# Local operand of a state-space mixer from half-row products of C, and quarter 3's first products moved ahead of the scan's end

## The chip, the cores and the metric

The kernel runs on one core of a Trainium2 chip. The metric is the device time of one execution in microseconds; a kernel is run several times and the median counts. Beside that, one execution is recorded by the hardware profiler, and all rows below come from that record of the kernel before.

## What is computed

The program is a small two-layer network on 256 tokens of width 2048, in float32: a state-space (S5) mixer with a gated projection, a feed-forward block, a dilated-window attention layer, and a second feed-forward block. The change lies in the mixer alone. Cut to what matters, it is, for each of 128 groups of 16 channels with 64 complex states:

```
def step(carry, u_c):                       # a chunk of the sequence
    bu = einsum('blgh,gph->blgp', u_c, bb)  # input into the states (complex)
    _, s = associative_scan(combine, (a, bu), axis=1)
    st = a_cum * carry + s                  # states over time
    y = einsum('blgp,ghp->blgh', st_re, cr) - einsum('blgp,ghp->blgh', st_im, ci)
    return st[:, -1], y
y = y + d_skip * u
g = gelu(y)
val, gate = split(g @ w_glu)
out = val * sigmoid(gate)
```

## The kernel before

The mixer handles the sequence as 64 short chunks of 4 tokens, and the 128 groups as four quarters (`qr` 0 to 3). Inside a chunk the answer is a fixed linear map of the chunk's own inputs, the *local operand* `mt`; across chunks a state is carried by a serial scan of 63 steps on VectorE (`scan`), one chain for quarters 0 and 1 (`sa`) and one for quarters 2 and 3 (`sb`). The output of a quarter is the sum of *local products* (`y_local`: inputs `ub` times `mt`) and *state products* (`y_state`: scanned states `sts` times `fds`, which GpSimd prepares), in two PSUM tiles. State products can be made for chunks 0 to 31 (early half) before the scan has ended, and for chunks 32 to 63 (late half) behind its end.

The work stands in one order written out by hand (`T`, `A`, `G`, `W` are TensorE, ScalarE, GpSimd and VectorE with that order kept). Every engine runs its own queue in order.

`build_m(qr)` makes a quarter of `mt`. It multiplies the taps `gps[qr]` (128 rows: two halves of 64, one for each half `y` of a pair of groups) with the output matrix `cp`, real and imaginary part in turn, and adds the skip term (`dsm`, through the identity `ident`). The two halves must not mix, so ScalarE first writes copies of `cp` in which the other half's rows are zero (`m_operand`, tile `cb`, through `masks`), and each product has 128 rows and 2 x 32 columns. ScalarE then copies the sum into `mt`, and SyncE sends six small transfers that shift it for the other three tokens of a chunk (line 477).

Behind it come the local products of quarters 0 and 1, their early state products, those of quarter 2, and then, as the chain goes on: late state products of quarters 0 and 1, gelu on ScalarE, a transpose (`turn`), a high and a low part of the result (`low`, VectorE), and the first products with the gated projection's weights (`feed`). `feed(1, 1)` is the last of those ahead of the end of `sb`; then late state products of quarter 2, all of quarter 3, and the rest.

PSUM is held in three pools: `ps_mm` (4 tiles), `ps_tr` (2), `ps_ms` (2). The scan keeps tables in two tiles of `ps_mm` until it has ended. Line 59 is the helper through which all ordered instructions pass, so tiles tell them apart, not lines.

Of the kernel before, what the change touches and what calls it, by code (L numbers as in the profile page):

```python
# [12 lines left out]
FP32 = mybir.dt.float32  # L13
F32R = mybir.dt.float32r
I32 = mybir.dt.int32
AF = mybir.ActivationFunctionType
# [4 lines left out]
P = 128  # L21
# [8 lines left out]
GI = 16  # L30
NS = 64
# [30 lines left out]
class Net:  # L62
# [141 lines left out]
    def s5_glu(self):  # L204
# [242 lines left out]
            for k in range(2):  # L447
                pair(cp[:, k, mo:mo + 16], cf[:, k, :, mo:mo + 16], ct[:, :, mo:mo + 16])

        def m_operand(qr, j4):  # L450
            m0 = 16 * qr + 8 * j4
            cb = early.tile([P, 2, 4, 2, 32], FP32, name="cb", tag="cb", bufs=2)
            src = cp[:, :, m0:m0 + 8].rearrange("p r (j x) o -> p r j (x o)", x=2)
            for y in range(2):
                A.activation(out=cb[:, :, :, y], in_=src, func=AF.Copy, scale=masks[:, y:y + 1])
            return cb

        def build_m(qr):
            cbs = [m_operand(qr, j4) for j4 in range(2)]
            ps = self.ps_ms.tile([P, 8, 2, 2, GI], FP32, name="ms")  # L460
            for xx in range(2):
                T.matmul(ps[:, :, :, xx], lhsT=self.ident,
                         rhs=dsm[:, 16 * qr:16 * qr + 16].rearrange("p (j y) o -> p j y o", y=2),
                         start=(xx == 0), stop=False, skip_group_check=True)
            for j in range(8):
                for ri in range(2):
                    T.matmul(ps[:, j], lhsT=gps[qr][:, ri, 2 * j:2 * j + 2].rearrange("p x s i -> p (x s i)"),
                             rhs=cbs[j // 4][:, ri, j % 4].rearrange("p y c -> p (y c)"),
                             start=False, stop=(ri == 1), skip_group_check=True)
            mo = 16 * qr  # L470
            for xx in range(2):
                r = slice(64 * xx, 64 * xx + 64)
                A.copy(out=mt[r, 3, mo:mo + 16].rearrange("p (j y) o -> p j y o", y=2), in_=ps[r, :, :, xx])
            for t in range(3):
                n = 16 * (t + 1)
                for xx in range(2):
                    nc.sync.dma_start(out=mt[64 * xx:64 * xx + n, t, mo:mo + 16],
                                      in_=mt[64 * xx + 64 - n:64 * xx + 64, 3, mo:mo + 16])
# [31 lines left out]
        def y_local(qr, pool, nm):  # L510
            pss = [pool.tile([P, 8, 4, GI], FP32, name=nm) for _ in range(2)]
            for jq in range(8):
                for y in range(2):
                    for xx in range(2):
                        T.matmul(pss[y][64 * xx:64 * xx + 64, jq],
                                 lhsT=ub[qr // 2][:, (qr % 2) * 8 + jq, y, xx],
                                 rhs=mt[:, :, 2 * (8 * qr + jq) + y],
                                 start=(jq == 0), stop=False, skip_group_check=True)
            return pss

        def y_state(qr, pss, jqs=range(8), c0=0, c1=64):
            st, mo = sts[qr // 2], 16 * (qr % 2)
            for jq in jqs:
                for ri in range(2):
                    for xx in range(2):
                        for y in range(2):
                            r = slice(64 * y, 64 * y + 64)
                            T.matmul(pss[y][64 * xx + c0:64 * xx + c1, jq],
                                     lhsT=st[r, c0:c1, ri, mo + 2 * jq + xx],
                                     rhs=fds[qr][r, :, ri, 2 * jq + xx],  # L530
                                     start=False, stop=(ri == 1), skip_group_check=True)
# [78 lines left out]
        def rest(c, half):  # L610
            r, hi, lo = ws[c, half]
            tt(lo, r, hi.bitcast(FP32), ALU.subtract, W)

        def feed(c, half):
            r, hi, lo = ws.pop((c, half))
            self.products(gb0, [(hi[:, k], lo[:, k]) for k in range(2)], lhs, T)
# [3 lines left out]
        def turn(qr, j4):  # L620
            if qr % 2 == 0 and j4 == 0:
                gtile[qr // 2] = self.act_tile()
                lhs.extend(gtile[qr // 2][:, k] for k in range(8))
            pt = self.ps_ms.tile([P, 4, 2, NS], FP32, name="ms")
            for t in range(4):
                T.transpose(out=pt[:, t], in_=gms[qr][:, j4, t].rearrange("p j y o -> p (j y o)"),
                            identity=self.ident)
            for xx in range(2):
                hi = lhs[4 * qr + 2 * j4 + xx][:, 0].rearrange("p (c t) -> p t c", t=4)
                A.copy(out=hi, in_=pt[:, :, xx])  # L630
            return pt
# [39 lines left out]
        feed(1, 0)  # L671
        high(2, 0)
        feed(1, 1)
        rest(2, 0)
        y_state(2, yl[2], range(8), 32, 64)
        high(2, 1)
        rest(2, 1)
        gms[2] = gelu(yl[2])
        yl[3] = y_local(3, self.ps_mm, "mm")
        y_state(3, yl[3])  # L680
        turns(2)
        gms[3] = gelu(yl[3])
        feed(2, 0)
# [333 lines left out]
```

## Time and profile before

| | |
|---|---|
| median of 3 runs | 2430.44 us (2430.07 to 2431.36) |
| profiled execution | 2428.69 us |
| its span | 2426.9 us |
| TensorE busy | 2392.5 us, 99% of the span |
| VectorE, ScalarE, GpSimd busy | 55%, 45%, 5% |

The span is the time from the first to the last recorded instruction; the profiled execution's own time has 1.8 us around it. A product of two float32 operands appears in the trace as two weight loads (LDWEIGHTS, engine row PEld) and two multiplications (MATMUL, row PE). A form such as `64*128 64x128` means a tile of the array of 64 rows and 128 columns, and an operand of 64 partitions and 128 elements.

### The profile page before, as it was taken

The numbers are of one execution on the slowest core, as the hardware profiler recorded it, in microseconds if no ns is written. First come the engines' busy times: TensorE is split into PE (matmuls) and PEld (weight loads), VectorE is DVE, ScalarE is ACT, GpSimd is POOL, SyncE is SP. The second block draws the span as 40 slices with busy tenths as digits, with TensorE's granted clock in tenths as the row PEclk, the third lists the DMA queues.
The fourth block names the chain that finished last, engine by engine and source line by source line (L and its number), as shares of the span: only waits on it lengthen the run. The fifth ranks groups of instructions, "written<-read, shape, count | busy, mean of one in ns | idle before, by whom it ended". The sixth has DMA issues, their size and how long they took to land.

```text
span 2426.9 us, 29373 instructions
## 1 busy us (share of the span) xinstructions
PE 2392.5 (99%) x11856; PEld 1936.8 (80%) x11856; DVE 1323.8 (55%) x1974; ACT 1081.4 (45%) x1367; POOL 113.5 (5%) x113
## 2 busy tenths in 40 slices
PE   6899999999999999999999999999999999999999
PEld 5788888888888888888888888788888888888887
DVE  8955454454444454565446676765454444454454
ACT  7344444444334444554445555554444433344433
POOL 4800000000000000000000000100000000000000
PEclk9899999999999999999999999999999999999999
DMA  2345555555555555555554444445555555555554
GB/s 85 96 163 185 181 189 180 185 191 176 189 191 187 179 188 182 182 194 181 184 184 170 156 156 142 156 154 185 182 188 179 185 191 187 184 184 188 179 197 148
DMA packets 63033, 423.58 MB, mean 175 GB/s; under 512 B 8112, under 2 KB 9520, under 8 KB 12336
## 3 DMA queue, kind: packets, MB, share of 16 engines
q1 hardware_dynamic: 61744, 419.60, 50.7%
q8 instruction: 93, 1.52, 0.3%
q10 hardware_dynamic: 1152, 2.10, 0.2%
q14 instruction: 44, 0.36, 0.0%
HBM read 418.79 MB, written 2.10 MB: 173 GB/s over the span
## 4 chain that ended last, share of the span: by engine, by line
PE 97%; DVE 2%; ACT 1%; issue 0%; DMA 0%; POOL 0%; SPq 0%; DVEq 0%; POOLq 0%
PE mm L122 30%; PE mm L124 30%; PE mm L123 30%; PE ms L59 2%; PE tr L59 1%; PE ms L857 1%; PE tr L743 1%; PE mm L59 1%; PE tr L808 1%; DVE mm L59 0%; PE tr L857 0%; PE tr L185 0%; DVE gp L59 0%; DVE gpb L59 0%; PE ms L887 0%
## 5 line engine op out<-in xcount | busy, mean ns | idle before, releaser
L104 DVE TENSOR_TENSOR wlo<-raw,whi 128x1024 fp32r<-128x1024 f32 x776 | 948.5, 1224 | 1003.6 <-ACT whi L103 1002.1
L103 ACT CAST whi<-raw 128x1024 fp32r<-128x1024 f32 x776 | 813.0, 1048 | 1161.9 <-PE mm L124 1142.2
L122 PE MATMUL mm<-whi,actt 128*128 128x512 f32 x3104 | 1235.8, 398 | 1.4 <-ACT whi L103 1.4
L124 PE MATMUL mm<-whi,actt 128*128 128x512 f32 x3104 | 1229.6, 396 | 0.0
L123 PE MATMUL mm<-wlo,actt 128*128 128x512 f32 x3104 | 1229.3, 396 | 0.0
L124 PEld LDWEIGHTS mm<-whi,actt 128*128 128x128 f32 x3104 | 583.1, 188 | 139.2
L122 PEld LDWEIGHTS mm<-whi,actt 128*128 128x128 f32 x3104 | 583.1, 188 | 138.3 <-ACT whi L103 2.1
L123 PEld LDWEIGHTS mm<-wlo,actt 128*128 128x128 f32 x3104 | 583.2, 188 | 136.9 <-DVE wlo L104 0.4
L795 POOL TENSOR_TENSOR sc<-ssq,mhalf 128x8 f32<-128x8 f32 x16 | 32.1, 2005 | 475.0 <-DVE ssq L793 475.0
L174 POOL TENSOR_TENSOR r<-m,mhalf 128x1 f32<-128x1 f32 x6 | 3.2, 552 | 1053.1 <-DVE m L173 848.9
L59 DVE TENSOR_TENSOR actr<-actr,mm 128x64 f32<-128x64 f32 x252 | 46.7, 215 | 2.0
L729 ACT ACTIVATE sg<-mm,r 128x512 f32<-128x512 f32 x44 | 30.1, 690 | 21.3 <-PE mm L124 21.0
L59 DVE TENSOR_TENSOR mm<-mm,actr 128x128 f32<-128x128 f32 x126 | 37.0, 294 | 0.9
L866 ACT ACTIVATE s<-s,mx 128x384 f32<-128x384 f32 (+1 forms) x32 | 24.8, 774 | 25.1 <-DVE mx L864 25.1
L59 POOL TENSOR_TENSOR fpr<-pf,cp 128x512 f32<-128x512 f32 x32 | 34.9, 1092 | 0.0
L733 DVE SCALAR_TENSOR_TENSOR sg<-mm,r,sg 128x512 f32<-128x512 f32 x44 | 30.9, 742 | 0.0
L59 ACT COPY actr<-ms 128x252 f32<-128x252 f32 (+1 forms) x40 | 19.9, 580 | 22.5 <-PE ms L59 21.4
L791 ACT ACTIVATE sq<-mm 128x512 f32<-128x512 f32 x32 | 19.0, 594 | 23.5 <-PE mm L124 23.5
L871 DVE SCALAR_TENSOR_TENSOR p<-s,z,p 128x128 f32<-128x128 f32 (+1 forms) x64 | 26.3, 411 | 3.8 <-ACT p L869 3.6
L747 DVE TENSOR_TENSOR actt<-tr,actt 128x512 fp32r<-128x512 f32 x44 | 28.2, 681 | 0.0
L746 ACT CAST actt<-tr 128x512 fp32r<-128x512 f32 x44 | 23.7, 590 | 10.1 <-PE tr L743 10.1
L743 PEld LDWEIGHTS tr<-ident,sg 128*128 128x128 f32 x176 | 19.4, 140 | 9.2 <-DVE sg L733 9.2
(180 smaller groups left out, 946.8 us busy)
## 6 DMA issues: line engine op xcount, KB each, us to landing
raw<-w_gu SPq DMA_DIRECT2D x176, 1024.0 KB, 4.8
raw<-w_down SPq DMA_DIRECT2D x88, 1024.0 KB, 4.8
raw<-w_q SPq DMA_DIRECT2D x48, 1024.0 KB, 4.8
raw<-w_glu SPq DMA_DIRECT2D x32, 1024.0 KB, 4.8
raw<-w_kv SPq DMA_DIRECT2D x32, 1024.0 KB, 4.7
raw<-w_o SPq DMA_DIRECT2D x16, 1024.0 KB, 4.7
actr<-x_c SPq DMA_DIRECT2D x2, 1024.0 KB, 6.4
xr<-x_t SPq DMA_DIRECT2D x8, 256.0 KB, 5.8
```

The costliest lines, as they stand in the source:

```text
L59: return lambda *a, **k: self.tc.keep_in_program_order(call(*a, **k))
L103: (scalar or self.nc.scalar).copy(out=hi, in_=r)
L104: (vector or self.nc.vector).tensor_tensor(out=lo, in0=r, in1=hi.bitcast(FP32), op=ALU.subtract)
L122: matmul(ps[th], lhsT=a[:, 0, ts], rhs=hi, start=(k == 0), stop=False)
L123: matmul(ps[th], lhsT=a[:, 0, ts], rhs=lo, start=False, stop=False)
L124: matmul(ps[th], lhsT=a[:, 1, ts], rhs=hi, start=False, stop=(k == n - 1))
L729: nc.scalar.activation(out=s, in_=ps[th], func=AF.Silu, scale=rs[th])
L733: nc.vector.scalar_tensor_tensor(out=sg[th], in0=ps[th], scalar=rs[th], in1=sg[th], op0=ALU.mult, op1=ALU.mult)
L743: nc.tensor.transpose(out=pt[:, k, th * P:(th + 1) * P], in_=sg[th][:, c:c + P], identity=self.ident)
L747: nc.vector.tensor_tensor(out=ht[:, k0:k0 + 2, 1], in0=pt, in1=ht[:, k0:k0 + 2, 0].bitcast(FP32), op=ALU.subtract)
L795: nc.gpsimd.tensor_tensor(out=sc, in0=ssq, in1=self.mhalf.rearrange("p (a b) -> p a b", a=2), op=ALU.pow)
L871: nc.vector.scalar_tensor_tensor(out=pr, in0=sc[:, g], scalar=z, in1=pr, op0=ALU.mult, op1=ALU.add)
```

## The change

`build_m` no longer uses masked copies. It takes each product over one half of the rows (64) with the 32 columns of `cp` that belong to it, and puts the two halves into two PSUM tiles, from `ps_ms` and `ps_tr` in turn. The skip term is added to each of the two. The result copies read both. Quarter 3's local products and its early state products, now in `ps_ms`, are written ahead of quarter 2's late state products; the transposes of quarters 2 and 3 use `ps_mm`.

```diff
-        def m_operand(qr, j4):
-            m0 = 16 * qr + 8 * j4
-            cb = early.tile([P, 2, 4, 2, 32], FP32, name="cb", tag="cb", bufs=2)
-            src = cp[:, :, m0:m0 + 8].rearrange("p r (j x) o -> p r j (x o)", x=2)
+        def build_m(qr):
+            pool, nm = ((self.ps_ms, "ms"), (self.ps_tr, "tr"))[qr % 2]
+            ps = [pool.tile([P, 8, 2, GI], FP32, name=nm) for _ in range(2)]
+            mo = 16 * qr
             for y in range(2):
-                A.activation(out=cb[:, :, :, y], in_=src, func=AF.Copy, scale=masks[:, y:y + 1])
-            return cb
-
-        def build_m(qr):
-            cbs = [m_operand(qr, j4) for j4 in range(2)]
-            ps = self.ps_ms.tile([P, 8, 2, 2, GI], FP32, name="ms")
-            for xx in range(2):
-                T.matmul(ps[:, :, :, xx], lhsT=self.ident,
-                         rhs=dsm[:, 16 * qr:16 * qr + 16].rearrange("p (j y) o -> p j y o", y=2),
-                         start=(xx == 0), stop=False, skip_group_check=True)
+                for xx in range(2):
+                    T.matmul(ps[y][:, :, xx], lhsT=self.ident,
+                             rhs=dsm[:, mo:mo + 16].rearrange("p (j y) o -> p j y o", y=2)[:, :, y],
+                             start=(xx == 0), stop=False, skip_group_check=True)
             for j in range(8):
                 for ri in range(2):
-                    T.matmul(ps[:, j], lhsT=gps[qr][:, ri, 2 * j:2 * j + 2].rearrange("p x s i -> p (x s i)"),
-                             rhs=cbs[j // 4][:, ri, j % 4].rearrange("p y c -> p (y c)"),
-                             start=False, stop=(ri == 1), skip_group_check=True)
-            mo = 16 * qr
+                    for y in range(2):
+                        r = slice(64 * y, 64 * y + 64)
+                        T.matmul(ps[y][:, j], lhsT=gps[qr][r, ri, 2 * j:2 * j + 2].rearrange("p x s i -> p (x s i)"),
+                                 rhs=cp[r, ri, mo + 2 * j:mo + 2 * j + 2].rearrange("p x o -> p (x o)"),
+                                 start=False, stop=(ri == 1), skip_group_check=True)
             for xx in range(2):
                 r = slice(64 * xx, 64 * xx + 64)
-                A.copy(out=mt[r, 3, mo:mo + 16].rearrange("p (j y) o -> p j y o", y=2), in_=ps[r, :, :, xx])
+                for y in range(2):
+                    A.copy(out=mt[r, 3, mo:mo + 16].rearrange("p (j y) o -> p j y o", y=2)[:, :, y],
+                           in_=ps[y][r, :, xx])
...
-            pt = self.ps_ms.tile([P, 4, 2, NS], FP32, name="ms")
+            pt = (self.ps_ms.tile([P, 4, 2, NS], FP32, name="ms") if qr < 2 else
+                  self.ps_mm.tile([P, 4, 2, NS], FP32, name="mm"))
...
         feed(1, 1)
+        yl[3] = y_local(3, self.ps_ms, "ms")
+        y_state(3, yl[3], range(8), 0, 32)
         rest(2, 0)
         y_state(2, yl[2], range(8), 32, 64)
         high(2, 1)
         rest(2, 1)
         gms[2] = gelu(yl[2])
-        yl[3] = y_local(3, self.ps_mm, "mm")
-        y_state(3, yl[3])
+        y_state(3, yl[3], range(8), 32, 64)
         turns(2)
```

The order of instructions shows it at two places. On TensorE, where the local operand is built, before (`gp_228` to `gp_231` are the taps of the four quarters; the last two rows are the local products of quarters 0 and 1):

```order
L59 MATMUL ms<-dsm,ident 128x16x16 x2
L59 MATMUL ms<-cb,gp_228 128x64 x16
L59 MATMUL ms<-dsm,ident 128x16x16 x2
L59 MATMUL ms<-cb,gp_229 128x64 x16
L59 MATMUL ms<-dsm,ident 128x16x16 x2
L59 MATMUL ms<-cb,gp_230 128x64 x16
L59 MATMUL ms<-dsm,ident 128x16x16 x2
L59 MATMUL ms<-cb,gp_231 128x64 x16
L59 MATMUL ms<-actr 64x64 x32
L59 MATMUL tr<-actr 64x64 x32
```

The same place on TensorE in the changed kernel:

```order
L59 MATMUL ms<-dsm,ident 128x8x16 x4
L59 MATMUL ms<-cp,gp_228 128x32 x32
L59 MATMUL tr<-dsm,ident 128x8x16 x4
L59 MATMUL tr<-cp,gp_229 128x32 x32
L59 MATMUL ms<-dsm,ident 128x8x16 x4
L59 MATMUL ms<-cp,gp_230 128x32 x32
L59 MATMUL tr<-dsm,ident 128x8x16 x4
L59 MATMUL tr<-cp,gp_231 128x32 x32
L59 MATMUL ms<-actr 64x64 x32
L59 MATMUL tr<-actr 64x64 x32
```

Sixteen products of 64 columns a quarter have become thirty-two of 32, and the quarters take turns in two pools.

On TensorE at the end of the scan (the first two rows are the end of `feed(1, 1)`; `mm<-actr 32x64` are the late state products of quarter 2, `ident,gm` its transposes), as a difference:

```order
 L59 MATMUL tr<-wlo,actt 128x512
 L59 MATMUL tr<-whi,actt 128x512
+L59 MATMUL ms<-actr 64x64 x32
+L59 MATMUL ms<-actr 32x64 x64
 L59 MATMUL mm<-actr 32x64 x64
-L59 MATMUL mm<-actr 64x64 x96
-L59 MATMUL ms<-ident,gm 128x128 x8
+L59 MATMUL ms<-actr 32x64 x64
+L59 MATMUL mm<-ident,gm 128x128 x8
```

Quarter 3's 32 local products and 64 early state products have moved ahead of quarter 2's late ones, and 64 late ones stay behind them in place of 64 whole ones.

## Rows read from the trace of the kernel before

**Rows 1.** The page: TensorE's busy time, share and instructions, and the shares of the chain that ended last by engine.

```profile
PE 2392.5 (99%) x11856; PEld 1936.8 (80%) x11856; DVE 1323.8 (55%) x1974; ACT 1081.4 (45%) x1367; POOL 113.5 (5%) x113
PE 97%; DVE 2%; ACT 1%; issue 0%; DMA 0%; POOL 0%; SPq 0%; DVEq 0%; POOLq 0%
```

**Rows 2.** The chain that ended last, in order of time, around the change: start in us, us, what.

```profile
62.16 3.80 PE ms L59 x32
...
73.29 13.86 PE ms L59 x68
...
87.99 3.47 PE ms L59 x60
...
97.22 3.24 issue
...
109.24 1.68 PE ms L59 x85
...
121.06 8.40 PE tr L59 x36
129.46 9.47 PE mm L59 x302
```

**Rows 3.** Stretches of time: their length, the busy time of each engine in them (and instructions), TensorE's granted clock, the share of the DMA engines and GB/s.

```profile
62.10:66.50 4.40, 4.34 (x36) 4.25 (x36) 4.40 (x30) 1.29 (x5) 4.24 (x6) 1.00 0.00 0
66.50:75.60 9.10, 7.37 (x59) 6.56 (x57) 9.10 (x61) 4.38 (x11) 8.71 (x11) 1.00 0.13 36
75.60:87.10 11.50, 11.50 (x52) 10.51 (x50) 11.50 (x76) 2.44 (x6) 11.00 (x13) 0.50 0.09 26
87.90:92.60 4.70, 4.61 (x86) 4.62 (x88) 4.70 (x31) 1.81 (x4) 4.47 (x5) 0.50 0.88 277
92.60:97.20 4.60, 4.60 (x209) 4.41 (x206) 4.60 (x31) 1.74 (x2) 4.43 (x6) 0.99 0.90 337
97.20:100.40 3.20, 0.02 (x1) 0.00 (x0) 3.20 (x22) 1.04 (x1) 3.04 (x4) 0.87 0.41 166
100.40:106.30 5.90, 5.84 (x149) 5.67 (x150) 5.73 (x36) 0.00 (x0) 5.67 (x8) 0.50 0.03 6
```

**Rows 4.** The building of the local operand: TensorE's waits for the masked copies (us in total, times, longest), ScalarE's copies by form (count, busy us, mean ns), and weight loads in a quarter at the full clock and in one at half (length, busy us, loads, granted clock).

```profile
PE ms L59 <- ACT cb L59: 2.3, 3, 0.9
...
L59 ACT ACTIVATE cb<-cp,masks 128x256 f32<-128x256 f32 x16 | 6.8, 497 | 0.1
L59 ACT COPY actr<-ms 64x256 f32<-64x256 f32 x8 | 2.9, 367 | 16.9 <-PE ms L59 16.8
...
62.16:65.80 3.64, 3.64 (x33) 1.00 0.00 0
80.05:87.07 7.02, 6.90 (x33) 0.50 0.09 26
```

**Rows 5.** Instructions in time: the last copies that free a PSUM tile for the local operand (ScalarE), and the skip term's products at the full and at half the clock.

```profile
60.36 1.05 ACT L59 COPY actr<-ms 128x252 f32<-128x252 f32 x2
60.47 1.10 PE L59 MATMUL ms<-dsm,ident 128*128 128x256 f32 x4
...
78.06 2.02 PE L59 MATMUL ms<-dsm,ident 128*128 128x256 f32 x4
```

**Rows 6.** Weight loads by form: transposes over 128 and over 64 rows; the first four loads of quarter 3's state products in time and as a group; quarter 3's local products (all rows, column halves in turn) and state products (row halves and column halves in turn), and quarter 2's late state products. Busy us, mean ns.

```profile
L59 PEld LDWEIGHTS tr<-ident,gp 128*128 128x128 f32 x21 | 2.3, 142 | 0.9 <-issue 0.9
L59 PEld LDWEIGHTS ms<-ident,actr 64*128 64x128 f32 x16 | 1.1, 139 | 0.0
...
134.06 0.23 PEld L59 LDWEIGHTS mm<-actr 64*64 64x64 f32 x4
...
L59 PEld LDWEIGHTS mm<-actr 64*64 64x64 f32 x4 | 0.2, 215 | 0.1
...
L59 PEld LDWEIGHTS mm<-actr 128*64 128x64 f32 x64 | 2.0, 138 | 0.1
L59 PEld LDWEIGHTS mm<-actr 64*64 64x64 f32 x128 | 4.7, 241 | 0.1
L59 PEld LDWEIGHTS mm<-actr 64*32 64x32 f32 x128 | 2.5, 167 | 0.4 <-issue 0.4
```

**Rows 7.** VectorE in time towards the end of the scan (a weight split, scan steps, the low parts of quarters 0 and 1 with the wait ahead of them in brackets, the last scan step), and TensorE's state products behind the chain's end.

```profile
107.78 1.32 DVE L59 TENSOR_TENSOR wlo<-raw,whi 128x1024 fp32r<-128x1024 f32 x1
...
114.07 0.47 DVE L59 TENSOR_TENSOR actr<-actr,mm 128x64 f32<-128x64 f32 x2
115.32 2.24 DVE L59 TENSOR_TENSOR actt<-ms,actt 128x256 fp32r<-128x256 f32 x4 [0.77 <-ACT actt L59]
...
122.29 2.21 DVE L59 TENSOR_TENSOR actt<-ms,actt 128x256 fp32r<-128x256 f32 x4 [0.49 <-ACT actt L59]
...
128.40 0.47 DVE L59 TENSOR_TENSOR actr<-actr,mm 128x64 f32<-128x64 f32 x2
...
129.39 2.83 PE L59 MATMUL mm<-actr 64*32 64x64 f32 x130
```

**Rows 8.** SyncE's queue where the local operand ends (the first weight chunk, then the last six shifting transfers), and ScalarE's gelu of quarter 2.

```profile
87.17 0.33 SPq L96 DMA_DIRECT2D raw<-w_glu  x1
87.60 3.69 SPq L477 DMA_DIRECT2D actr<-actr  x6
...
132.13 1.21 ACT L59 ACTIVATE gm<-mm 128x256 f32<-128x256 f32 x4 [4.34 <-PE mm L59]
```

## The prediction

> **What bounds the kernel now.** I read the profile in this order. First the page's busy shares and its chain line: TensorE is busy 99% of the span and carries 97% of the chain that ended last [rows 1]. So any time that TensorE gains or loses early in the kernel shifts everything behind it by as much, and nothing behind it can make that good. Second the chain in order of time around the change, 59 to 139 us [rows 2]: the four quarters of the local operand run from 62.16 to 87.1, the products that use it start at 87.99, the late state products of quarter 0 at 109.24, the work after the end of the scan chain at 129.46. The reader is to see that nearly every piece is a TensorE piece, with one stall of 3.24 us at 97.22 that nothing in the profile explains ("issue"). Third the clock by stretches [rows 3]: full (1.00, 2.4 GHz) up to 75.6, half (0.50, 1.2 GHz) from 75.6 to 92.6, and half again from 100.4 to 106.3, behind the stall. Fourth VectorE's scan in time [rows 7]: it runs without a pause to 114.54, waits 0.77 us for ScalarE's rounded gelu tile at 115.32 and 0.49 us at 122.29, and ends its last step at 128.87. TensorE starts the state products that need this end at 129.39, straight behind the weight products ahead of them. So at the chain's end neither engine waits for the other by more than half a microsecond.
>
> **The change, part by part.** Masked copies: 16 ScalarE instructions of 497 ns go, 6.8 us of ScalarE. On the path they count only as TensorE's three waits for them, 2.3 us in all [rows 4]. The eight result copies of 0.37 us become sixteen of half the width; they stand behind each quarter's last product, while TensorE is in the next quarter in another pair of buffers, so I cost them at nothing. Without that cover they would cost four copies, about 1 us, a quarter. Behind the last quarter they hold back the products of quarter 1 alone, for which quarter 0's are ahead; that takes the 0.9 us between 87.1 and 87.99 away.
>
> Products: a quarter has 16 now, which the trace shows as 32 weight loads and 32 multiplications. It will have 32 products, so 64 loads of 128 columns, each over 64 rows. What a product costs now is its load: 33 loads take 3.64 us at the full clock and 7.02 us at half, 0.110 and 0.213 us each [rows 4]. A load over half the rows is not shorter: 139 ns for 64 rows, 142 ns for 128 in the transposes [rows 6]. The Trainium skill, "TensorE: Matmul & The Clock Gate", section "LDWEIGHTS (loading the stationary operand)", says the same, that the load goes by columns and not by rows; by that rule alone the change doubles each quarter.
>
> So everything hangs on whether the loads of the two row halves run side by side. The trace has no 128-column load of this kind, so I bound it. Lower bound: two at a time, 0.055 us a load at full clock and 0.107 at half. Upper bound: one at a time, 0.110 and 0.213. The nearest rows are the state products of quarter 3, which do alternate between the row halves (and between two halves of the columns): their first four loads, 215 ns each, all lie within 0.23 us, so row halves do load together; but 128 of them took 4.7 us, 0.037 us for 64 columns, where the products over all rows took 2.0 us for 64, 0.031 us [rows 6]. Scaled to 128 columns, 0.037 is 0.073. I take 0.065 at full clock, between 0.055 and 0.073, and 0.110 at half, where the load itself is so slow that a shared path should be enough. A quarter is then 64 x 0.065 = 4.2 us or 64 x 0.110 = 7.0 us, against 3.8 and 7.1 today: the split wins nothing on TensorE. The Trainium skill, "TensorEngine Tiling (Array Packing)", section "Key Properties", says that different tiles of the array load and multiply in parallel; the four loads in 0.23 us agree.
>
> D-skip products: four with 128 columns in place of two with 256, 8 loads x 0.110 = 0.9 us, and 1.7 at half; today 1.10 and 2.02 with their tail [rows 5]. No difference worth a term. A quarter now wants two buffers at once, and the second is freed by the last scan-input copy, which ends at 61.41 [rows 5]; half of the D-skip products come behind it, so the first product starts at about 61.9, not 62.16.
>
> Clock: before it fell at 75.6 TensorE did these products, with pauses for ScalarE. It came back at 92.6 in the products behind them [rows 3]. The new stream has no pauses, but each multiplication passes half the columns through half the rows. No row tells when the clock falls in such a stream. I take 68, one quarter and a bit in; 65 and never are the bounds.
>
> Sum: 61.9 + 4.2 = 66.1; D-skip to 67.0; by 68 some 15 of the second quarter's loads; the other 49 at 0.110 take it to 73.4; two more quarters of 1.7 + 7.0 make 90.8. The next products start there, not at 87.99: **+2.8 us**.
>
> The hoist: quarter 3's local products (2.0 us) and the early half of its state products go ahead of the late state products of quarter 2. They would save 4.5 us if TensorE waited for the chain's end. It does not: its weight products end at 129.46 [rows 2] and the chain ended at 128.87. So the order changes and the sum does not, except that the state products are now two halves of 2.5 us instead of one piece of 4.7 [rows 6]: **+0.3 us**. The gelu of quarter 2, 1.21 us on ScalarE [rows 8], was covered by 7 us of TensorE and is now covered by 2.5.
>
> The queue: the first weight chunk, issued at 87.17 ahead of six small transfers that take SyncE 3.69 us, now goes behind them [rows 8]. Its first reader on the path is VectorE's split at 107.78 [rows 7]; 4 us later is still early. I cost it at nothing; without that slack it costs the 3.7 us.
>
> Total +3.1 us. The profiled execution took 2428.69 us (span 2426.9), so its sum is 2431.8; the median of the runs, 2430.44, is 1.75 us higher, and against it I forecast **2433.5 us**.
>
> **Rivals.** *The clock holds.* Four quarters at 4.2 and three D-skips at 0.9 end at 81.4, and the next products start 6.6 us early. That gain is not kept: VectorE's order has the low parts of quarter 0 behind scan steps that end at 114.54, and its two waits, 0.77 + 0.49, are all that an early TensorE can take out. With the 0.3 above, -1.0: 2429.4. For it: no pauses. Against it: the clock fell in a stream with longer multiplications. The same end comes if the stall at 97.22 goes away, since a gain is capped by the same two waits.
>
> *Loads one at a time* (the other side). 7.0 us for the first quarter, 13.6 at half: the first ends at 69.8, three more of 1.7 + 13.6 at 115.7, +28: 2458.4. This is what the load rule of the Trainium skill's page gives without any overlap. The four loads of [rows 6] speak against it; that 64-column loads over half the rows are no cheaper than over all rows speaks for it. The point from which the change is slower by more than 0.2% is 0.120 us a load at half clock, only a little over my 0.110.
>
> *Loads at the scaled price of the state products,* 0.073 and, if it goes with the clock, 0.147: the start moves to 98.6, +10.9: 2441.3.
>
> *The stall lasts twice as long:* the weight chunks are now issued together, in the middle of this work; +3.2 on the forecast, 2436.7.
>
> **How the numbers follow.** Forecast 0.48; clock holds 0.18; stall gone 0.07; stall doubled 0.07; scaled price 0.08; one at a time 0.12. The forecast's own range is that of the clock's fall: at 65 the start is 93.0, +5.3 (2435.7); as late as today it is early, capped at -1.0 (2429.4). For all cases 2428.8 to 2442 leaves out the one-at-a-time loads and some scatter at the low end. A measurement of this kernel tells about 0.2%, 4.9 us. No case gains that: 0.03 for what I have not seen. Slower by more: one at a time, scaled price, doubled stall and a tenth of the forecast, 0.32. Same: 0.65.
>
> **What would show it.** In the profile after, the start of quarter 0's local products (87.99 now) gives the sum: about 91 if I am right, 81 if the clock held, beyond 98 if the loads don't overlap. The distance between the products' loads gives the price directly, and the granted clock from 62 to 95 the rest. At the chain's end TensorE should have no wait ahead of the late state products of quarter 2. I would be wrong if the work behind the chain shrinks by 4 us with TensorE idle ahead of it, or if the weight products from 117 to 129 wait longer for their chunks.

## The result and the profile after

The changed kernel took 2437.53 us (median of 6 runs, 2436.37 to 2439.94), the kernel before beside it 2430.26 us (6 runs, 2428.04 to 2434.26). The ratio is 1.0031, 95% interval 1.0021 to 1.0042: slower by 0.31%, +7.3 us where +3.1 was forecast. The profiled execution took 2438.57 us, its span 2436.8 us against 2426.9. The time stands in two places.

The page after, to be read beside [rows 1]: TensorE's busy time and instructions, the shares of the chain, and the queue that brings instructions.

```profile
PE 2400.8 (99%) x12128; PEld 1943.5 (80%) x12128; DVE 1324.1 (54%) x1974; ACT 1075.3 (44%) x1359; POOL 113.5 (5%) x113
PE 97%; DVE 2%; ACT 1%; issue 0%; DMA 0%; POOL 0%; SPq 0%; DVEq 0%; POOLq 0%
q8 instruction: 95, 1.56, 0.3%
```

TensorE is still the bound, with 8.3 us more of busy time and 272 more multiplications (and as many loads).

The chain that ended last, in order of time, after (start, us, what), beside [rows 2]:

```profile
61.34 5.85 PE ms L59 x68
67.19 8.97 PE tr L59 x72
...
85.14 8.97 PE tr L59 x72
94.12 3.61 PE ms L59 x64
...
102.74 2.66 issue
...
123.78 3.06 PE tr L59 x12
...
136.12 4.24 PE ms L59 x177
...
141.81 2.37 issue
...
146.37 1.27 issue
...
149.33 1.07 ACT actt L59 x2
```

The same view of the kernel before, at two places that [rows 2] doesn't hold (the first weight products, and ScalarE's copies behind the last state products):

```profile
117.11 3.07 PE tr L59 x12
...
139.55 1.07 ACT actt L59 x2
```

Four marks tell where the span grew. Quarter 0's local products start at 94.12 instead of 87.99: **+6.1**. The first weight products start at 123.78 instead of 117.11: +6.7, so 0.5 came in between. The late state products start at 136.12 instead of 129.46: still +6.7. The copies behind the last of them start at 149.33 instead of 139.55: +9.8, so another **+3.1** came there, where the chain now has two gaps of 2.37 and 1.27 us that the profile lays to nothing but "issue". From there on the two executions run in parallel (the spans differ by 9.9). The medians differ by less, since before's profiled execution lay 1.57 us under the median given above and the one of after 1.04 us over its own.

The front by stretches after, as in [rows 3]; the last row is the first of the two gaps at the end:

```profile
62.00:64.00 2.00, 2.00 (x36) 2.00 (x38) 0.00 (x0) 1.00 0.00 0
...
65.00:67.20 2.20, 2.20 (x23) 2.14 (x21) 2.20 (x16) 0.00 (x0) 2.04 (x4) 0.50 0.00 0
...
85.10:94.10 9.00, 9.00 (x76) 8.71 (x74) 9.00 (x60) 0.84 (x4) 8.61 (x11) 0.50 0.09 25
...
99.80:102.70 2.90, 2.90 (x147) 2.86 (x146) 2.90 (x20) 0.00 (x0) 2.82 (x4) 1.00 0.91 356
...
141.80:144.20 2.40, 0.03 (x4) 0.02 (x3) 0.00 (x0) 0.00 (x0) 0.00 (x0) 1.00 0.05 17
```

The first of these rows counts only the instructions that touch the taps. It shows the price of a half-row load at the full clock: 38 in 2.00 us, 0.053 us each, two at a time. The clock is at half from 64 to beyond 94, over 30 us; before it was 17 us ([rows 3], 75.6 to 92.6). And the gap at 141.8 has 5% of DMA beside it: other transfers fill the DMA engines up to there (0.99 of them from 141.0 to 141.8), but not while the gap lasts.

### The profile page after: what moved, and what is told of

The parts are those of the page before. It is cut to its first block, busy times and chain, and to the rows that moved or that the text cites. A ratio compares the mean times of both kernels' runs of the same rounds, so it can differ in the third digit from the quotient of the medians.

```text
span 2436.8 us, 29914 instructions
## 1 busy us (share of the span) xinstructions
PE 2400.8 (99%) x12128; PEld 1943.5 (80%) x12128; DVE 1324.1 (54%) x1974; ACT 1075.3 (44%) x1359; POOL 113.5 (5%) x113
## 4 chain that ended last, share of the span: by engine, by line
PE 97%; DVE 2%; ACT 1%; issue 0%; DMA 0%; POOL 0%; SPq 0%; DVEq 0%; POOLq 0%
PE mm L122 30%; PE mm L123 30%; PE mm L124 30%; PE tr L59 2%; PE ms L59 1%; PE ms L856 1%; PE tr L742 1%; PE tr L807 1%; DVE mm L59 0%; PE tr L856 0%; PE tr L185 0%; DVE gp L59 0%; PE mm L59 0%; DVE gpb L59 0%; PE ms L886 0%
## 5 line engine op out<-in xcount | busy, mean ns | idle before, releaser
L742 PE MATMUL tr<-ident,sg 128*128 128x128 f32 x176 | 26.7, 274 | 0.0
```

The source lines that it names most:

```text
L742: nc.tensor.transpose(out=pt[:, k, th * P:(th + 1) * P], in_=sg[th][:, c:c + P], identity=self.ident)
```

## The experiments

**The change in its two parts.** The first run has the new local operand with the old order behind it, the second the old local operand with the moved products.

```diff
 e1_build_only, against the kernel before: build_m as in the changed kernel, nothing else
 e2_tail_only, against the kernel before (the transposes of quarters 2 and 3 in ps_mm, as in the changed kernel):
...
+        yl[3] = y_local(3, self.ps_ms, "ms")
+        y_state(3, yl[3], range(8), 0, 32)
         rest(2, 0)
         y_state(2, yl[2], range(8), 32, 64)
...
-        yl[3] = y_local(3, self.ps_mm, "mm")
-        y_state(3, yl[3])
+        y_state(3, yl[3], range(8), 32, 64)
```

Expected of the first: 

> Half-row products in the local operand, everything behind them as in the kernel before. Theory: two costs that add. In the changed kernel quarter 0's local products start at 94.05 us instead of 87.99, +6.1, because the clock is at half from 64 on; the other +3.7 stands in two gaps of 2.37 and 1.27 us in the last state products, where TensorE waits for nothing that is recorded, and belongs to the moved products alone. Then here: start at 94.05, no gap over 0.5 us between the end of the weight products and the last state product, total +6.1 to +6.9 us. Rival: the build sets when the weight chunks and everything else run, so the gaps at the end come from it as well: +9 to +10 us and both gaps present.

Expected of the second: 

> Masked copies and the products over all rows as in the kernel before; only quarter 3's local and early state products ahead of the chain's end. Theory: the split of quarter 3's state products into two halves adds 64 products, each two loads and two multiplications, 256 instructions for TensorE in a stream in which a product is over in 0.04 us, and they come no faster than they are delivered: gaps of together 3 to 4 us behind 129.5 us, total +3.1 us. Rival: the gaps belong to the later place in time of the changed kernel; then no gaps, and +0.3 us or less.

Measured: the build alone 2435.75 us against 2430.21 (ratio 1.0020, interval 1.0011 to 1.0029), +5.5; the moved products alone 2431.68, +1.5 (1.0014, 1.0006 to 1.0023). Together +7.0, against +7.3 for the whole change: the medians add, in part by luck, since each of them moves by 1 or 2 us with the clock in front (below). The traces are the better ground. The chain of the build alone:

```profile
94.23 3.61 PE ms L59 x64
...
135.57 3.06 PE mm L59 x133
...
146.24 1.07 ACT actt L59 x2
```

The median is a little under the +6.1 to +6.9 expected, the profiled execution, 2435.37, is 6.7 over that of before. The start is that of the changed kernel, 94.23, and from the late state products to the copies it takes 10.7 us, against 10.1 before and 13.2 in the changed kernel: no large gap (0.34 and 0.17 us). The chain of the moved products alone:

```profile
128.51 3.90 PE ms L59 x159
...
135.09 1.62 issue
...
139.32 0.85 issue
...
141.62 1.07 ACT actt L59 x2
```

13.1 us, with gaps of 1.62 and 0.85, from a start no later than in the kernel before (128.51 against 129.46). So the gaps don't hang on the later place in time; but the median is +1.5 and not +3.1, since another thing differs between executions, the clock in front, taken up below.

**Is it the order or the number of instructions?** Two more runs take the moved part apart: the local products alone ahead, with the state products whole; and nothing moved, but the state products cut in two where they stand.

```diff
 e3_local_ahead, against e2_tail_only:
-        y_state(3, yl[3], range(8), 0, 32)
...
-        y_state(3, yl[3], range(8), 32, 64)
+        y_state(3, yl[3])
 e4_split_in_place, against the kernel before:
-        y_state(3, yl[3])
+        y_state(3, yl[3], range(8), 0, 32)
+        y_state(3, yl[3], range(8), 32, 64)
```

Expected of the first: 

> As the last one, but only quarter 3's 32 local products go ahead of quarter 2's late state products; its state products stay whole, 64, behind them. TensorE gets as many instructions as in the kernel before. Theory of the added instructions: no gap over 0.5 us behind 129.5, total within 0.5 us of the kernel before. Rival, the order alone (quarter 2's results, its gelu and its transposes come later): +3 us.

Expected of the second: 

> Nothing is moved: quarter 3's state products are written as two halves, chunks 0 to 31 and then 32 to 63, at the place they have in the kernel before, behind the chain's end. Theory of the added instructions: gaps of 3 to 4 us in this stream as in the changed kernel, total +2.5 to +4 us. Rival, the order: only the price of the two halves, 2 x 2.5 instead of 4.7 us, +0.3 us, no gaps.

Measured: the order alone 2430.13 us, -0.1 (1.0004, 0.9995 to 1.0013); the cut alone 2433.06, +2.9 (1.0018, 1.0010 to 1.0027). What TensorE waited for between the weight products and the copies (engine, what, by what: us in total, times, longest): the changed kernel,

```profile
PE mm L59 <- issue: 2.4, 1, 2.4
...
PE ms L59 <- issue: 1.3, 1, 1.3
```

the cut in place,

```profile
PEld mm L59 <- issue: 3.8, 4, 1.9
PE mm L59 <- issue: 2.9, 2, 1.8
```

and the order alone, whose only such row is

```profile
PEld ms L59 <- issue: 0.6, 2, 0.4
```

So it is the cut and not the move. The cut puts 64 products more into the stream, 256 instructions; the instruction queue counts in packets of just that: in the kernel before it had

```profile
q8 instruction: 93, 1.52, 0.3%
```

for 2 x 11,856 TensorE instructions, and 95 for 2 x 12,128 after: 255 instructions, 16.4 KB, a packet. Once a dense stretch of the changed kernel has had its first gap, one comes with each such packet. TensorE's multiplications in time, after:

```profile
105.40 3.18 PE L59 MATMUL tr<-fdx,actr 64*32 64x64 f32 x111 [2.66 <-issue]
...
110.15 3.27 PE L59 MATMUL mm<-actr 128*64 128x64 f32 x127 [0.95 <-issue]
114.14 0.90 PE L59 MATMUL mm<-actr 64*32 64x64 f32 x37 [0.73 <-issue]
...
117.87 1.13 PE L59 MATMUL ms<-fdx,actr 64*32 64x64 f32 x49 [1.36 <-issue]
```

From gap to gap there are 127 to 128 multiplications and as many loads, and 4.8, 4.0 and 3.7 us (3.5 between the two gaps at the end): the rate at which the packets come. The packets' own times show the link. In the trace of the changed kernel the instruction queue starts one at 103.0, 107.7, 111.8 and 115.5 us, and at 141.9 and 145.3, and TensorE goes on 2.3 to 2.5 us behind each of these six. In the traces of all the other kernels here, every wait of its multiplications laid to "issue" from 85 to 150 us ends in the same way, 2.2 to 2.9 us behind the start of a packet. State products in halves need 2.5 us for as many; the whole ones of [rows 6] need 4.7 us, which is slower than the packets. That is why cutting them costs the gaps and 2 x 2.5 us was not their price. The Trainium skill, "Runtime: NRT & Kernel Launch", section "Instruction fetch mechanics", describes blocks of 16 KiB, 256 instructions, and calls their fetch mostly hidden. The block agrees with the rows above; here it is not hidden where 256 instructions are over in 2.5 us.

**The clock and the columns.** Was it the half rows, or the small multiplications? This run passes 64 columns through each half-row product where the change passes 32; the loads are the same.

```diff
 e5_wide, against e1_build_only:
-            ps = [pool.tile([P, 8, 2, GI], FP32, name=nm) for _ in range(2)]
+            ps = [pool.tile([P, 8, 4, GI], FP32, name=nm) for _ in range(2)]
...
-                        T.matmul(ps[y][:, j], lhsT=...
-                                 rhs=cp[r, ri, mo + 2 * j:mo + 2 * j + 2].rearrange("p x o -> p (x o)"),
+                        n = 4 if mo + 2 * j < 62 else 2
+                        T.matmul(ps[y][:, j, 0:n], lhsT=...
+                                 rhs=cp[r, ri, mo + 2 * j:mo + 2 * j + n].rearrange("p x o -> p (x o)"),
```

Expected: 

> The local operand of the changed kernel, everything behind it as before, but each half-row product passes 64 columns of the output matrix through its half of the rows instead of 32 (the 32 that belong to the next pair go into columns of the PSUM tile that nobody reads; the last pair of quarter 3 stays at 32). The loads stay the same. Theory: in these kernels the granted clock follows what the multiplications pass through the array. With 32 columns it was at half from 64 to 98 us in both profiled executions that have them; with all rows and 64 columns it fell at 71 to 94. Twice the columns then bring back a later fall: the local products of quarter 0 start at 78 to 86 us instead of 94, median within 2 us of the kernel before. Rival: the clock follows something that the columns don't change (the half rows, or the place in time): start at 94, +5.5 us as with 32 columns.

Measured: 2428.95 us against 2429.30 (0.9997, 0.9988 to 1.0006). TensorE in time:

```profile
62.08 3.79 PE L59 MATMUL ms<-cp,gp 64*128 64x64 f32 x64
...
76.50 3.76 PE L59 MATMUL tr<-cp,gp 64*128 64x64 f32 x64
80.19 2.08 PE L59 MATMUL ms<-actr 128*64 128x64 f32 x64
...
105.00 3.66 PE L59 MATMUL ms<-fdx,actr 64*32 64x64 f32 x128 [5.35 <-DVE actr L59]
```

and two of its stretches:

```profile
62.10:65.80 3.70, 3.70 (x66) 3.63 (x65) 3.70 (x25) 0.00 (x0) 3.54 (x5) 1.00 0.02 4
...
76.50:80.10 3.60, 3.60 (x65) 3.60 (x64) 3.60 (x24) 0.00 (x0) 3.44 (x5) 1.00 0.18 50
```

With twice the work in each multiplication the same 256 loads are done at 80.2 instead of 94.2: the clock stayed at 1.00 through all four quarters. So the half rows as such do not bring the clock down; the narrow products did. The rows show a second thing: of the 14.0 us won in front against the build alone 6.8 arrive at the end, and of the 7.8 won against the kernel before nearly nothing, because TensorE then waits 5.35 us for the scan chain of quarters 0 and 1 at 105.00.

**Two loads at a time.** The same products in another order.

```diff
 e9_one_half_first, against e1_build_only:
-            for j in range(8):
-                for ri in range(2):
-                    for y in range(2):
+            for y in range(2):
+                for j in range(8):
+                    for ri in range(2):
```

Expected: 

> The local operand of the changed kernel, but in each quarter all 16 products of the first row half and then all 16 of the second, instead of the two in turn. Theory: the loads of the changed kernel ran in pairs, 0.0525 us a load at the full clock and 0.107 at half, only because neighbours are in different row halves. Here neighbours are in the same half: 0.110 and 0.213 us a load, 64 of them 13.6 us a quarter at half, start of quarter 0's local products at 119 us or later, +25 us or more. Rival: the price goes by rows, and two loads of 64 rows are never dearer than one of 128: no change against the changed kernel, start at 94.

Measured in one execution: 2459.3 us, +30. A quarter of 64 loads at half the clock in this run, and where the local products of quarter 0 start:

```profile
73.84 13.03 PE L59 MATMUL tr<-cp,gp 64*128 64x32 f32 x64
...
116.73 3.43 PE L59 MATMUL ms<-actr 128*64 128x64 f32 x64
```

and the same quarter in the changed kernel:

```profile
69.13 7.04 PE L59 MATMUL tr<-cp,gp 64*128 64x32 f32 x64
```

13.03 and 7.04 us: neighbours in different row halves load side by side, neighbours in one half do not. One at a time a load over 64 rows takes 0.204 us, little less than the 0.213 of one over 128 [rows 4], which is why the start is 116.7 and not beyond 119. The Trainium skill, "TensorE: Matmul & The Clock Gate", section "LDWEIGHTS (loading the stationary operand)", has the load go by columns alone; these two numbers agree, to 4%. The overlap comes from the order of two loops.

**The whole change with 64 columns.** This joins the cure for the front to the moved products.

```diff
 e11_after_wide, against the changed kernel: build_m as in e5_wide
```

Expected: 

> The changed kernel with one edit: 64 columns instead of 32 in each half-row product, as in the wide run. Theory of two separate costs: the front's cost goes (start of quarter 0's local products at 80 instead of 94), the gaps of the added instructions behind the chain's end stay, 2.5 to 3.6 us. Median +1.5 to +3 us against the kernel before. Rival: TensorE that is early in front has slack for the moved products, and the change brings what it was written for: -1 us or better.

Measured: 2431.28 us against 2429.47, +1.8 (1.0005, 0.9996 to 1.0014). That interval holds "no change"; at equal mean clock, 0.996, the four executions took 2431.0 to 2432.0 and ten of the kernel before 2427.4 to 2429.5. Its chain has the gaps of the changed kernel still:

```profile
134.28 2.08 issue
...
138.55 1.27 issue
```

The front's cost is gone and the end's is not: two separate costs, as the first two runs said.

**What can be won.** The next runs ask what the front's time is worth, and whether the two ideas of the change help where they don't cost instructions or clock. The first leaves the products as before and makes the masked copies a quarter earlier; the second moves quarter 3's local products and cuts 256 instructions (quarter 1's state products in one piece).

```diff
 e6_copies_ahead, against the kernel before:
-            cb = early.tile([P, 2, 4, 2, 32], FP32, name="cb", tag="cb", bufs=2)
+            cb = early.tile([P, 2, 4, 2, 32], FP32, name="cb", tag=("cb", "gt")[qr % 2], bufs=2 + qr % 2)
...
-            cbs = [m_operand(qr, j4) for j4 in range(2)]
+            cbs = cb_next.pop(qr)
...
+            if qr < 3:
+                cb_next[qr + 1] = [m_operand(qr + 1, j4) for j4 in range(2)]
...
+        cb_next = {0: [m_operand(0, j4) for j4 in range(2)]}
 e8_whole1_local_ahead, against e3_local_ahead:
-        for qr in range(2):
-            y_state(qr, yl[qr], range(8), 0, 32)
+        y_state(0, yl[0], range(8), 0, 32)
...
-        y_state(1, yl[1], range(4), 32, 64)
+        y_state(1, yl[1], range(4))
...
-        y_state(1, yl[1], range(4, 8), 32, 64)
+        y_state(1, yl[1], range(4, 8))
```

Expected of the first: 

> The kernel before with its masked copies, but ScalarE makes those of the next quarter while TensorE is in this one (buffers of a second ring), so TensorE's three waits of 0.7 to 0.9 us for them go away. Theory: TensorE reaches quarter 0's local products 2.3 us earlier at the same clock, and about as much again where the clock then holds longer; but what it gains is kept only as far as VectorE waits for it later, 0.77 + 0.49 us. Median -1 us, at most -2. Rival: the waits cost nothing because the front is bound elsewhere: 0.

Expected of the second: 

> Before's local operand; quarter 3's local products ahead of quarter 2's late state products; and quarter 1's state products in one piece, 64, behind its scan chain's end instead of two halves of 64 each: 256 instructions fewer for TensorE. Theory of the added instructions, turned round: the gap of 3.24 us ahead of 100.46 gets shorter by 2 us or more, and with quarter 3's local products as work that does not wait for VectorE about 1 to 3 us of it are kept: -1 to -3 us. Rival: the gap comes from the weight chunks' transfers that start then and stays: 0.

Measured: 2428.10 us (0.9992, 0.9983 to 1.0001) and 2428.93 (0.9996, 0.9987 to 1.0005), beside 2429.30 before: neither can be told from no change. The multiplications of the first,

```profile
79.99 1.97 PE L59 MATMUL ms<-actr 128*64 128x64 f32 x60 [0.58 <-ACT actr L59]
...
104.94 3.65 PE L59 MATMUL ms<-fdx,actr 64*32 64x64 f32 x128 [4.45 <-DVE actr L59]
```

and of the second:

```profile
96.18 3.09 PE L59 MATMUL mm<-actr 128*64 128x64 f32 x127 [3.28 <-issue]
...
105.00 3.52 PE L59 MATMUL ms<-fdx,actr 64*32 64x64 f32 x128 [4.38 <-DVE actr L59]
```

Each starts quarter 0's local products earlier than 87.99 (79.99 and 83.45) and then waits over 4 us for the same scan chain at 105. The second expectation failed: -0.4 us instead of -1 to -3, and a gap of 3.28 us stands there with 256 instructions less. This first gap of the stream comes in kernels with and without the cut, and why it is the longest is not settled. The rival of that expectation, the weight chunks' transfers, fits the traces. With 0.94 to 1.00 of the DMA engines busy the instruction queue's packet starts after TensorE has stopped (103.0 against 102.74 in the changed kernel, 98.3 against 97.22 in the one before, 93.8 against 92.91 here). With 0.01 or 0.02 of them busy it starts 1.0 to 1.6 us ahead of the stop (111.8 against 113.42, 115.5 against 116.51 and 145.3 against 146.37 in the changed kernel). No run took the chunks away, so this isn't shown.

Then VectorE's order behind 105, the next bound: the low part of quarter 0 two scan steps earlier, with the copies ahead, and the local products ahead; the same with the half-row products of 64 columns; and last, quarter 1's low part earlier too.

```diff
 e10_best, against e6_copies_ahead, with the local products moved as in e3_local_ahead:
-        steps(2, sb)
         pts = [turn(0, j4) for j4 in range(2)]
...
             low(0, j4, pts[j4])
-        steps(2, sb)
+        steps(4, sb)
 e12_wide_best: the same, with build_m as in e5_wide
 e13_both_low, against e10_best:
-        steps(4, sb)
+        steps(2, sb)
...
         feed(0, 1)
-        steps(2, sb)
         for j4 in range(2):
             low(1, j4, pts[j4])
```

Expected of the first: 

> The kernel before with the masked copies made a quarter ahead (as in the run before), quarter 3's local products alone moved ahead of quarter 2's late state products, and on VectorE the low part of quarter 0 ahead of two scan steps instead of behind them. There TensorE waited for VectorE: 4.45 us ahead of the late state products of quarter 0, and at 127.4 it began the late products of quarter 2 straight at the chain's end. Theory: with the clock held in front, VectorE's order sets the time up to 127.4; the weight products begin 1.7 us earlier (two steps of 0.84), and the 2.0 us of local products fill what TensorE would wait for the chain's end. 2426.0 to 2427.2 us, 1 to 2 below the run with the copies ahead alone. Rival: the low part waits for ScalarE's rounded tile anyway: as the run with the copies ahead, 2428.

Expected of the second: 

> The same as the first run of this call, but with the half-row products of 64 columns in the place of the masked copies. Theory: both keep the clock in front, so both are bound by VectorE behind it: within 1 us of the first run, 2426 to 2428 us. Rival: 64 loads in place of 32 bring the instruction gaps forward and cost 2 us.

Expected of the third: 

> The run with copies ahead, local products ahead and the low part of quarter 0 earlier, and now the low part of quarter 1 earlier too: four scan steps less stand ahead of it on VectorE (they run behind it). In the last such run TensorE got its early start back as a wait: its products stood at 121.78 behind that low part, which began at 121.12. Theory: VectorE's chain still ends at 127.4, TensorE's weight products run through from 114.4 and end near 125.6, the 2.0 us of local products fill the time to the chain's end, and the late products of quarter 2 start with 2 us less behind them: 2426 to 2427.3 us. Rival: the low part then waits for ScalarE's copies of the transposes, and nothing is gained: 2428 to 2429.5.

Measured: 2429.31 (0.9998, 0.9989 to 1.0007) and 2428.68 us (0.9998, 0.9990 to 1.0007), both without effect against 2429.47, where 2426 to 2428 had been expected; then 2426.16 us against 2429.24, ratio 0.9986, interval 0.9977 to 0.9995. The first of the three in its chain, where the wait went:

```profile
121.12 0.62 DVE actt L59
121.78 5.52 PE tr L59 x22
127.31 2.02 PE ms L59 x64
```

TensorE started its weight products earlier and then stood at VectorE's next low part, so the local products began where the chain of scan steps ended anyway. Two short "issue" gaps, 0.18 and 0.74 us, also stand behind the chain's end, in a stream without the cut. With that part earlier as well:

```profile
113.66 0.50 PE L59 MATMUL tr<-whi,actt 128*128 128x512 f32 x1 [1.29 <-ACT gm L59]
128.85 2.62 PE L59 MATMUL mm<-actr 64*32 64x64 f32 x128 [0.84 <-DVE actr L59]
137.47 0.50 PE L59 MATMUL tr<-whi,actt 128*128 128x512 f32 x1 [0.26 <-ACT actt L59]
```

No wait stands between 113.66 and 128.85, the local products are done by then, and the work behind the chain's end is 8.6 us long, against 10.0 in the first of the three; 0.9 of the difference are its two gaps, which are gone. This version beats the kernel before by 3.1 us and, by the difference of each to before, the changed one by about 10. At a mean clock of 0.996, where five of its executions and six of the kernel before can be compared, the gain is 2.8. It keeps the idea of the second half of the change, without the cut; which of its four edits the gain needs was not run.

**The clock differs between executions.** In the profiled executions of the kernels with all rows and 64 columns the clock fell at different times in front: at 71.4 in the cut in place, at 75.6 in the kernel before and not until beyond 92 in the run with the copies ahead. The cut in place has the front of the kernel before, instruction for instruction, and its profiled execution shows what the clock alone can cost there. It was at half also from 54.4 to 57.8, where the kernel before had it at full, and quarter 0's local products start 5.1 us later than at 87.99:

```profile
93.06 3.47 PE ms L59 x60
```

This execution, mean clock 0.991, took 2438.57 us; four others of the same kernel with a mean of 0.993 took 2432.2 to 2432.9. The mean granted clock of the whole execution tells the same of runs without a trace. Of 32 executions of the kernel before beside the first four runs, the 15 with a mean of 0.995 or more took 2427.3 to 2430.7 us, the 11 with 0.992 or less 2430.7 to 2435.6. All 6 of the changed kernel and all 10 of the build alone had 0.992 or less; all 11 with the copies ahead and all 10 of the wide run had 0.994 or more. So a part of the executions of the kernel before already pays what the changed kernel always pays, and a median over few of them moves by 1 or 2 us. That is why the moved products alone gave +1.5 in the median: at equal clock, 0.996, its four executions took 2430.9 to 2432.5 and ten of before 2428.0 to 2430.7, some 2.5 us.

## Why the prediction was right and wrong

The time, 2437.53, is in the range, and the sign of the forecast's +3.1 is right; it is 4 us too small in the medians and 6.7 in the traces (+9.8), in two terms, the clock's and the halves'. So the place in the range is in part luck. The range's upper end stood for dearer loads (2441.3), which did not come, and the measured time lies beyond what the forecast gave for any fall of the clock, 2429.4 to 2435.7. By the prediction's own measure of 0.2% the outcome is "slower by more", which had 0.32, and not "same", which had 0.65: the whole interval, 1.0021 to 1.0042, lies above it.

*Masked copies:* right. No piece of ScalarE stands in the chain between 61.34 and 94.12; the sixteen narrower copies are hidden.

*Half-row loads:* the mechanism is right and the price a little too high at the full clock: 0.053 us measured for 0.065 taken, at half 0.110 (a quarter 7.04 us, 7.0 forecast). Two loads do run at a time, at about the lower bounds of 0.055 and 0.107; a quarter wins nothing. The rival without overlap was priced at 2458.4, and the run with the loops changed took 2459.3.

*Skip term:* a quarter and its four products take 8.97 us at half where 8.7 was counted; 0.8 over three quarters, which the cheaper loads of the first quarter give back in part.

*The clock:* this term was mis-sized. The fall was put at 68, with 65 as the early bound, and came at 64, with some 40 loads done. By the prediction's own working the start is 90.8 for 68 and 93.0 for 65, so about 93.7 for 64; measured 94.12. The +2.8 was +6.1. Even the early bound was too late. The prediction wrote that no row told when the clock falls in such a stream, but it had named what speaks for an early fall, each multiplication passing half the columns through half the rows, and took 68 all the same. The wide run shows that the columns were it: with the same half rows the clock held. The rival in which the clock holds was priced at 2429.4, its gain capped by VectorE; the wide run took 2428.95, capped by VectorE at an earlier place, the 5.35 us at 105.00. So the prediction's opening, that any time TensorE gains or loses early shifts everything behind it, held for the loss and not for the gain.

*The hoist:* that it saves nothing is right: TensorE's weight products ended at 136.12, and no wait for the scan stands behind them. That the two halves cost 0.3 is the second failed term: +3.1 in the trace, +2.9 in the run with the cut alone, and the prediction had no term for the arrival of instructions. The price of a half, 2.5 us, was read from a row in which 64 products in halves stood alone behind weight products, which are few and long; here three dense pieces follow each other. The row that could have told was in [rows 2]: the stall of 3.24 us that "nothing in the profile explains" stands in a dense stream of state products in halves. The prediction took it for a thing of the weight chunks, and priced a rival on that (the stall twice as long). It did not double at its place (2.66 us after); its kind came back at the end. That the weight chunks have a part in it is still possible (above), but it ends 2.2 us behind the start of a queue packet, like the others.

*The queue:* right; VectorE's first split starts at 107.71, as before at 107.78.

*What would show it:* the start of the local products was named as the sum of the front, about 91 if right. At 94 it fell between the forecast and the rival of 98.6, and the granted clock, named for the rest, told why.

## What to carry to other kernels

Before cutting products into smaller ones, count instructions as well as loads: 256 of TensorE's took 3.5 us or more to arrive here, so a stream that is done with them in 2.5 us gets gaps that no wait explains. A split over row halves is free for loads as long as neighbours alternate, but narrow products can leave the clock at half for tens of microseconds, and twice the columns cost only some 0.2 us a quarter under the same loads (3.60 us for 64 of them, where 0.053 each make 3.4). And where the granted clock of one stretch differs between executions, compare them at equal mean clock before believing a median.

## What the runs showed that was not expected

Doing useless work won time: the same 256 loads with 64 columns instead of 32 were over at 80.2 instead of 94.2 us, with the clock at 1.00 instead of 0.50.

A gap labelled "issue" with an idle DMA beside it (5% from 141.8 to 144.2) follows the packets of the instruction queue, 255 instructions each: it ends 2.3 us behind the start of one.

Two scan steps more or less ahead of one instruction on VectorE decided nothing in one place (2429.31) and, moved ahead of the next such instruction as well, 3 us (2426.16). The wait that was taken out had moved to the next late instruction in VectorE's queue, and the gain came only once that was early too; 0.9 us of it in the traces are two "issue" gaps.
